# The second layer's feed-forward up projection by seven products instead of eight, with weight sums formed in DRAM

## The chip, the core and the metric

The kernel runs on one core of a Trainium2 chip. The metric is the device time of one execution in microseconds, lower is better; the kernel before has a median of 3490.95 us over three runs (3489.8 to 3501.07).

## What is computed

One inference step of a two-layer decoder trunk, for 1024 prompt tokens and 8 x 8 sample tokens (1088 in all, `NT`). Each layer mixes tokens, adds an output projection, and adds a gated feed-forward part with a causal convolution over three tokens on the gate. All arrays are float32. The part that the change touches is this one, and the first layer's copy of it runs beside the new weight sums:

```python
D_MODEL = 1024; D_FF = 2816; CONV_W = 3

def conv_glu(xn, conv_prev, w_up, conv_w, conv_b, w_down):
    T = xn.shape[1]
    u = xn @ w_up                                   # w_up: 1024 x 5632
    gate, val = u[..., :D_FF], u[..., D_FF:]
    ext = jnp.concatenate([conv_prev.astype(gate.dtype), gate], axis=1)
    conv = conv_b
    for j in range(CONV_W):
        conv = conv + ext[:, j:j + T] * conv_w[j]
    h = jax.nn.silu(conv) * val
    return h @ w_down, ext[:, T:]

# in trunk, for each layer l
        x = x + jnp.concatenate([o_tok, o_mem], axis=-1) @ P['w_o'][l]
        f, c = conv_glu(rms_norm(x, P['norm_ffn'][l]), conv0[l], P['w_ffn_up'][l],
                        P['conv_w'][l], P['conv_b'][l], P['w_ffn_down'][l])
        x = x + f
    y = rms_norm(x, P['final_norm'])
```

## The kernel before

The activations stay in SBUF with channels on partitions: `s.x` is 8 blocks (`KC`) of 128 channels by 1088 tokens. Every float32 product is made of three TensorE (PE) products: both operands are split into a rounded high part (fp32r) and a remainder, and `gemm_y` (L468 to L476) issues, for each block k of 128 input channels, wh·xh (L474), wh·xl (L475) and wl·xh (L476), all into one PSUM tile. The tokens are walked in three groups `G3` of 364, 364 and 360 columns, one PSUM bank each.

Weights come by `load_w` (L195 to L209): one DMA of 128x512 (256 KB) on SyncE's queue (SP, L204) into a ring `wr` of three buffers, a rounding copy `wh` on ScalarE (ACT, L207), and the remainder `wl` on VectorE (DVE, L208) into rings of four. An SP row waits until its `wr` buffer is free, and all weight loads stand in one line on SP.

`trunk_tail(l)` (from L1405) is the same code for both layers: output projection with w_o (loads of `od`, the attention's output in DRAM, through GpSimd's queue at L1427, split at L1433 and L1434), norm, `ffn` (from L1247), and for layer 1 `final`, the last norm with transposes and stores. The layers are numbered 0 and 1 in the code; the words "first" and "second" layer are used here. In `ffn` the 2816 hidden channels are 22 chunks c of 128. `up(c)` makes gate and value of a chunk (8 blocks x 3 groups x 3 products each), copies the gate from PSUM into `ext` (L1278), applies the convolution (L1300 to L1302), SiLU (L1303), the product with the value (L1317) and the split of the hidden tile into `hh` and `hl` (L1130, L1131). `down(i)` multiplies a group of three or four chunks by the down weights and adds to `s.x` (L1159); it is interleaved with the `up` of the following chunks (a merge by numbers of steps: 24 of `down` against 110 of `up`), and the last group runs alone in token pieces of 416, 416 and 256 in the second layer, beside `final`. Outside the few stretches marked for manual order, a scheduler sets each engine's order from the order of the code and an estimate of its own. Layers are run one after the other, with the second layer's attention between them: `trunk_tail(0)`, `attention`, `trunk_tail(1)`.

## Time and profile before

| | |
|---|---|
| median of three runs | 3490.95 us |
| the profiled execution | 3513.38 us |
| its span | 3511.6 us |
| PE busy | 3368.6 us (96%) |
| DVE, ACT, POOL busy | 1790.5, 1298.7, 457.7 us |
| first layer's feed-forward part | from about 1100 to 1840 us |
| second layer's last part (output projection to the end) | 2594.2 to 3511.6 us |

The profile is of one execution that took 3513.38 us, 0.6% above the median; shares and durations are read from it. It is read by stages: windows give the busy time of every engine in a stretch, and the waits of PE say what it lacked. Starts of successive matmuls are more exact than their durations, since ends of pipelined matmuls are modelled.

### The profile page before, as it was taken

Reading aid. Unit: us, or ns where it says so; the run is one execution under the profiler, and the core shown is the slowest. Engines: PE = TensorE matmul, PEld = TensorE weight load, DVE = VectorE, ACT = ScalarE, POOL = GpSimd, SP = SyncE. Lnnn points to the kernel's source line nnn. Section 1 sums busy time; section 2 is a strip of 40 time slices with the busy share of each in tenths; the row PEclk is TensorE's granted clock in tenths of the full one; section 3 lists DMA queues with packets and bytes.
Section 4 is the critical chain, followed back from the end, with each engine's and each line's share of the span. In section 5 each row is a group of like instructions: output and inputs, shape, how many; then the busy total and the mean of one; then the engine's idle time right before and its main releaser. Section 6 shows DMA issues by size and latency. Waiting matters only on the chain. (4 is left out here: it accounts for less than half of the span.)

```text
span 3511.6 us, 58202 instructions
## 1 busy us (share of the span) xinstructions
PE 3368.6 (96%) x23112; PEld 2899.4 (83%) x23112; DVE 1790.5 (51%) x4242; ACT 1298.7 (37%) x2971; POOL 457.7 (13%) x767
## 2 busy tenths in 40 slices
PE   6999999999889999999999999899999999999998
PEld 5555677775579999999999888655579999999998
DVE  5776676775535343333345477434445433343344
ACT  5555445543544222212225455333334312222222
POOL 4323133331011000000003001011111000000000
PEclk9998699998889999999999999899999999999999
DMA  4212011113141111111113102345321111111112
GB/s 119 56 39 76 22 39 41 38 47 95 51 153 48 43 49 43 43 46 46 44 46 111 53 28 70 123 163 179 121 75 42 49 49 40 46 46 43 47 44 78
DMA packets 299284, 227.13 MB, mean 65 GB/s; under 512 B 40890, under 2 KB 278222, under 8 KB 294916
## 3 DMA queue, kind: packets, MB, share of 16 engines
q1 hardware_dynamic: 285220, 166.82, 16.3%
q0 software_dynamic: 9888, 51.93, 4.2%
q10 hardware_dynamic: 3904, 4.65, 0.4%
q8 instruction: 182, 2.98, 0.3%
q14 instruction: 90, 0.74, 0.1%
HBM read 197.59 MB, written 25.76 MB: 64 GB/s over the span
## 5 line engine op out<-in xcount | busy, mean ns | idle before, releaser
L474 PE MATMUL pmm<-xh,wh 128*128 128x364 f32 (+2 forms) x2664 | 882.3, 331 | 7.5 <-ACT wh L207 4.8
L476 PE MATMUL pmm<-xh,wl 128*128 128x364 f32 (+2 forms) x2664 | 875.1, 328 | 0.0
L475 PE MATMUL pmm<-xl,wh 128*128 128x364 f32 (+2 forms) x2664 | 872.9, 328 | 0.3
L474 PEld LDWEIGHTS pmm<-xh,wh 128*128 128x128 f32 (+1 forms) x2664 | 500.1, 188 | 12.4 <-ACT wh L207 5.1
L475 PEld LDWEIGHTS pmm<-xl,wh 128*128 128x128 f32 (+1 forms) x2664 | 500.6, 188 | 3.0 <-DVE xl L1434 0.8
L476 PEld LDWEIGHTS pmm<-xh,wl 128*128 128x128 f32 (+1 forms) x2664 | 500.8, 188 | 1.4 <-DVE wl L208 0.2
L207 ACT CAST wh<-wr 128x512 fp32r<-128x512 f32 (+3 forms) x399 | 238.5, 603 | 561.1 <-PE pmm L475 333.4
L208 DVE TENSOR_TENSOR wl<-wr,wh 128x512 fp32r<-128x512 f32 (+2 forms) x307 | 205.0, 670 | 369.9 <-ACT wh L207 369.3
L1159 DVE TENSOR_TENSOR x<-x,pdn 128x364 f32<-128x364 f32 (+1 forms) x240 | 127.4, 531 | 419.2 <-PE pdn L476 419.2
L476 PE MATMUL pdn<-hh,wl 128*128 128x364 f32 (+1 forms) x912 | 300.2, 329 | 0.0
L475 PE MATMUL pdn<-hl,wh 128*128 128x364 f32 (+1 forms) x912 | 298.7, 328 | 0.0
L474 PE MATMUL pdn<-hh,wh 128*128 128x364 f32 (+1 forms) x912 | 298.3, 327 | 0.0
L474 PE MATMUL pmm<-xn,wh 128*128 128x292 f32 (+2 forms) x552 | 207.0, 375 | 3.7 <-DVE e L504 3.7
L475 PE MATMUL pmm<-xn,wh 128*128 128x292 f32 (+2 forms) x552 | 196.9, 357 | 0.0
L476 PE MATMUL pmm<-xn,wl 128*128 128x292 f32 (+2 forms) x552 | 195.5, 355 | 0.6 <-POOL wl L208 0.6
L1278 ACT COPY ext<-pmm 128x364 f32<-128x364 f32 x132 | 58.7, 444 | 364.0 <-PE pmm L476 364.0
L1304 POOL COPY cout<-ext 128x2 f32<-128x2 f32 x44 | 16.9, 385 | 1261.2 <-ACT ext L1278 1261.2
L476 PEld LDWEIGHTS pdn<-hh,wl 128*128 128x128 f32 x912 | 171.3, 188 | 1.1
L475 PEld LDWEIGHTS pdn<-hl,wh 128*128 128x128 f32 x912 | 171.3, 188 | 0.0
L474 PEld LDWEIGHTS pdn<-hh,wh 128*128 128x128 f32 x912 | 171.2, 188 | 0.0
L208 POOL TENSOR_TENSOR wl<-wr,wh 128x512 fp32r<-128x512 f32 (+1 forms) x92 | 121.7, 1325 | 195.9 <-ACT wh L207 163.8
L474 PEld LDWEIGHTS pmm<-xn,wh 128*128 128x128 f32 (+1 forms) x552 | 106.5, 193 | 27.9 <-issue 11.0
(720 smaller groups left out, 5984.1 us busy)
## 6 DMA issues: line engine op xcount, KB each, us to landing
wr<-in_w_ffn_up SPq DMA_DIRECT2D x176, 256.0 KB
wr<-in_w_in_a SPq DMA_DIRECT2D x84, 256.0 KB
wr<-in_w_ffn_down SPq DMA_DIRECT2D x64, 256.0 KB
wr<-in_w_o SPq DMA_DIRECT2D x32, 256.0 KB
wr<-in_w_ffn_down SPq DMA_DIRECT2D x32, 192.0 KB
xl<-odp POOLq DMA_DIRECT2D x4, 1456.0 KB
e<-in_x_prompt SPq DMA_DIRECT2D x16, 256.0 KB
out_y_p<-xl SPq DMA_DIRECT2D x8, 512.0 KB
```

The lines of the kernel that those rows point to most:

```text
L207: nc.scalar.copy(wh[:, :n, :m], wr[:, :n, :m])
L208: s.wl_eng.tensor_tensor(wl[:, :n, :m], wr[:, :n, :m], wh[:, :n, :m].bitcast(F32), ALU.subtract)
L474: nc.tensor.matmul(ps[:m, :n], wh[:, :m], xh[:, c0:c0 + n], start=(k == 0), stop=False)
L475: nc.tensor.matmul(ps[:m, :n], wh[:, :m], xl[:, c0:c0 + n], start=False, stop=False)
L476: nc.tensor.matmul(ps[:m, :n], wl[:, :m], xh[:, c0:c0 + n], start=False, stop=(k == last))
L1159: nc.vector.tensor_tensor(xv, xv, p[:, :n], ALU.add)
L1278: nc.scalar.copy(ext[:, 2 + c0:2 + c0 + m], p[:, :m])
L1304: nc.gpsimd.tensor_copy(cout[:, c, 0:2], ext[:, 1024:1026])
```

## The change

Write the up weights of the second layer as four quarters: the upper and the lower 512 input channels of gate and value, g1, g2, v1, v2 (each 512 x 2816), and cut the normed activations x in the same way into an upper part of four blocks (k = 0 to 3) and a lower one (k = 4 to 7), and the tokens of a half (`HT` = 544) into two quarters (`QT` = 272). The product of such a two-by-two arrangement takes eight quarter products. The change makes it from seven, with sums and differences of quarters as operands, and sums of the seven results (Winograd's form of Strassen's method).

- **Weight sums** (`sum_weights`, after L1247). Four arrays of 512 x 2816 in DRAM: vg = v1 + g1, gg = g1 + g2, vgg = vg + g2, all = vgg + v2. Each is made by four plain DMAs (rows in 128s, 1.44 MB each) on SP's queue that copy the first term, and four accumulating DMAs on GpSimd's queue that add the second. The 32 DMAs are stepped along the chunks of the first layer's `ffn`, one after an even chunk and two after an odd one.
- **Operands** (`combine_x`). For each half and each j of 0 to 3 the two normed blocks j and j + 4 (two DVE instructions of 544 columns), four differences on GpSimd (POOL, 272 columns), and the split of seven operands (seven ACT copies and seven DVE differences of 272). The first half's run beside the output projection, the second half's beside `down(0, 4)`.
- **Up** (`up` in `Seven`). 22 chunks x 2 halves, each seven products of 4 blocks x 3 matmuls of 272 columns. Seven weight tiles of 128x512 per chunk and half (`load_up`: three plain quarters, four sums from DRAM) through a ring `wa` of seven, with rings of five for the split parts. The results are put together from PSUM by two ACT copies, five DVE and two POOL instructions of 272. Convolution, SiLU, value product and split then run on 544 columns, with the first of the three convolution steps on ACT.
- **Output projection and down** run over quarters of 272 columns instead of three groups, down in groups of 4, 4, 4, 5 and 5 chunks per half, so the down weights are loaded once per half. The last `down` and `final` are walked by quarters of the second half.
- The first layer's own arithmetic is not changed. The new DMAs stand in its queues.

```diff
--- before.py
+++ after.py
+HT = NT // 2
+QT = NT // 4
+G4 = [(QT * i, QT) for i in range(4)]
...
+    def sum_weights(s, l):
+        nc, W = s.nc, s.I["w_ffn_up"][l]
+        S = s.wsum[l] = {z: s.t(s.dp, [512, DFF], f"ws{l}{z}", 1) for z in ("vg", "gg", "vgg", "all")}
+        def move(z, src, **kw):
+            eng = nc.gpsimd if kw else nc.sync
+            for r in range(0, 512, 128):
+                s.tc.keep_in_program_order(eng.dma_start(out=S[z][r:r + 128], in_=src[r:r + 128], **kw))
+                yield
+        def add(z, src):
+            return move(z, src, accum_op=ALU.add, max_dma_last_dim=5632)
+        g1, g2, v1, v2 = (W[r:r + 512, f:f + DFF] for f in (0, DFF) for r in (0, 512))
+        yield from s.seq(move("vg", v1), move("gg", g1), add("vg", g1), add("gg", g2), move("vgg", S["vg"]),
+                         add("vgg", g2), move("all", S["vgg"]), add("all", v2))
...
         groups = [(0, 4), (4, 4), (8, 4), (12, 4), (16, 3), (19, 3)]
+        sums = s.sum_weights(1)
...
                 yield from up(c, hs[i])
+                if l == 0:
+                    for _ in range(1 + c % 2):
+                        next(sums, None)
...
-        s.trunk_tail(1, od, xd, None, xst)
+        Seven(s).trunk_tail(1, od, xd, None, xst)
+
+
+class Seven(Step):
...
+    def residual(s, d, g, p, acc):
+        nc = s.nc
+        c0, n = g
+        xv = s.x[:, d, c0:c0 + n]
+        nc.vector.tensor_tensor(xv, xv, p[:, :n], ALU.add)
+        if acc is None:
+            return
+        a = acc[c0]
+        if d == 0:
+            nc.scalar.activation(a, xv, AF.Square)
+        else:
+            sq = s.st([128, QT], "nt", s.ntb)
+            nc.scalar.activation(sq[:, :n], xv, AF.Square)
+            nc.gpsimd.tensor_tensor(a, a, sq[:, :n], ALU.add)
...
+    def combine_x(s, h, gain, xs):
+        nc = s.nc
+        xs += [s.new_xq() for _ in range(7)]
+        lo, hi = slice(0, QT), slice(QT, HT)
+        for j in range(4):
+            a = []
+            for k in (j, j + 4):
+                a.append(s.st([128, HT], "tw", 2))
+                nc.vector.scalar_tensor_tensor(a[-1], s.x[:, k, HT * h:HT * h + HT], s.pv(gain[0], gain[1] + k), s.rstd[h], ALU.mult, ALU.mult)
+            yield
+            t = [s.st([128, QT], "nt", s.ntb) for _ in range(4)]
+            nc.gpsimd.tensor_tensor(t[0], a[0][:, hi], a[0][:, lo], ALU.subtract)
+            nc.gpsimd.tensor_tensor(t[1], a[1][:, hi], t[0], ALU.subtract)
+            nc.gpsimd.tensor_tensor(t[2], a[0][:, hi], a[1][:, hi], ALU.subtract)
+            nc.gpsimd.tensor_tensor(t[3], a[1][:, lo], t[1], ALU.subtract)
+            src = (a[0][:, lo], t[1], t[0], t[2], t[3], a[1][:, hi], a[1][:, lo])
+            for (xh, xl), z in zip(xs, src):
+                s.split(xh[:, j], xl[:, j], z)
+                yield
...
+    def gemm_x(s, wf, xs, h, acc=None, tag="dn"):
+        for d in range(KC):
+            w = wf(d)
+            for i in range(2):
+                p = s.pst(tag)
+                s.drain(s.gemm_y(p, w, xs[i], 0, QT))
+                s.residual(d, G4[2 * h + i], p, acc)
...
+    def load_up(s, l, c, first=False):
+        nc, W = s.nc, s.I["w_ffn_up"][l]
+        fv, fg = DFF + 128 * c, 128 * c
+        S = s.wsum[l]
+        for i, (src, r, f) in enumerate(((W, 0, fv), (S["vgg"], 0, fg), (S["gg"], 0, fg), (S["vg"], 0, fg), (W, 512, fg), (S["all"], 0, fg), (W, 512, fv))):
+            w = s.t(s.wp, [128, 4, 128], "wr", 3) if first and i < 3 else s.st([128, 4, 128], "wa", s.WA)
+            nc.sync.dma_start(out=w, in_=src[r:r + 512, f:f + 128].rearrange("(k p) f -> p k f", p=128))
+            wh, wl = (s.t(s.up, [128, 4, 128], z, 5, F32R) for z in ("uh", "ul"))
+            nc.scalar.copy(wh, w)
+            nc.vector.tensor_tensor(wl, w, wh.bitcast(F32), ALU.subtract)
+            yield [(wh[:, k], wl[:, k]) for k in range(4)]
...
+        def up(h, c, xs, out):
+            ws = s.load_up(l, c, h == c == 0)
+            ext = s.st([128, EW], "ext", 1)
+            es = ext[:, EW - 80:].rearrange("p (b t) -> p b t", t=10)
+            if h:
+                nc.gpsimd.tensor_copy(ext[:, 0:2], cout[:, c, 0:2])
+                nc.gpsimd.tensor_copy(es[:, :, 0:2], cprev[:, c].rearrange("p (b j) -> p b j", j=2))
+            else:
+                nc.gpsimd.memset(ext[:, 0:2], 0.0)
+            def product(i):
+                p = s.pst("mm")[:, :QT]
+                w, (xh, xl) = next(ws), xs[i]
+                for k in range(4):
+                    wh, wl = w[k]
+                    nc.tensor.matmul(p, wh, xh[:, k], start=k == 0, stop=False)
+                    nc.tensor.matmul(p, wh, xl[:, k], start=False, stop=False)
+                    nc.tensor.matmul(p, wl, xh[:, k], start=False, stop=k == 3)
+                    yield
+                return p
+            nt = lambda: s.st([128, QT], "nt", s.ntb)
+            add = lambda eng, o, a, b, op=ALU.add: eng.tensor_tensor(o, a, b, op)
+            V, P = nc.vector, nc.gpsimd
+            p = yield from product(0)
+            t1 = nt()
+            nc.scalar.copy(t1, p)
+            p = yield from product(1)
+            u2 = nt()
+            add(V, u2, p, t1, ALU.subtract)
+            p = yield from product(2)
+            t5 = nt()
+            nc.scalar.copy(t5, p)
+            p = yield from product(3)
+            u3 = nt()
+            add(V, u3, p, u2)
+            if h:
+                m = NP_ - 3 * QT
+                add(P, ext[:, 2 + QT:2 + QT + m], u3[:, :m], t5[:, :m])
+                b8 = lambda z: z[:, m:].rearrange("p (b t) -> p b t", t=8)
+                add(P, es[:, :, 2:10], b8(u3), b8(t5))
+            else:
+                add(P, ext[:, 2 + QT:2 + HT], u3, t5)
+            p = yield from product(4)
+            add(V, ext[:, 2:2 + QT], p, u3)
+            add(P, t5, t5, u2)
+            L = EW - 2 if h else HT
+            cv = s.st([128, EW], "cv", 1)[:, :L]
+            w = [s.pv(f"conv_w{l}{j}", c) for j in range(3)]
+            nc.scalar.activation(cv, ext[:, 0:L], AF.Identity, scale=w[0], bias=s.pv(f"conv_b{l}", c))
+            nc.vector.scalar_tensor_tensor(cv, ext[:, 1:1 + L], w[1], cv, ALU.mult, ALU.add)
+            nc.vector.scalar_tensor_tensor(cv, ext[:, 2:2 + L], w[2], cv, ALU.mult, ALU.add)
+            nc.scalar.activation(cv, cv, AF.Silu)
+            if h:
+                nc.gpsimd.tensor_copy(cout[:, c, 0:2], ext[:, EW - 82:EW - 80])
+                nc.gpsimd.tensor_copy(cout[:, c, 2:18].rearrange("p (b j) -> p b j", j=2), es[:, :, 8:10])
+            else:
+                nc.gpsimd.tensor_copy(cout[:, c, 0:2], ext[:, HT:HT + 2])
+            t = s.st([128, HT], "tw", 2)
+            p = yield from product(5)
+            add(V, t[:, QT:], p, t5, ALU.subtract)
+            p = yield from product(6)
+            add(V, t[:, :QT], p, t1)
+            hh, hl = s.st([128, HT], "hh", 7, F32R), s.st([128, HT], "hl", 7, F32R)
+            out.append((hh, hl))
+            if h:
+                V.tensor_tensor(t[:, :QT + m], cv[:, :QT + m], t[:, :QT + m], ALU.mult)
+                sv = s.bc(cv[:, EW - 80:EW - 79], [10, 8], [1, 8])
+                V.tensor_tensor(b8(t[:, QT:]), sv, b8(t[:, QT:]), ALU.mult)
+            else:
+                V.tensor_tensor(t, cv, t, ALU.mult)
+            s.split(hh, hl, t)
+            yield
...
+        groups = [(0, 4), (4, 4), (8, 4), (12, 5), (17, 5)]
+        hs, acc0, squares = {}, {}, []
...
+        def ups(h, i):
+            c0, n = groups[i]
+            hs[h, i] = []
+            if h and i == 0:
+                yield from s.combine_x(1, ("norm_ffn", 8 * l), operands[1])
+            for c in range(c0, c0 + n):
+                if h == 0 and c == 1:
+                    normed()
+                if h == 0 and c == 4:
+                    earlier()
...
+                yield from up(h, c, operands[h], hs[h, i])
...
+        def down(h, i):
+            yield from s.gemm_x(lambda d: wd(i, d), quarters(hs.pop((h, i))), h)
...
+        order = [(h, i) for h in range(2) for i in range(len(groups))]
+        for n, z in enumerate(order):
+            u = ups(*z)
+            if n:
+                s.merge([(down(*order[n - 1]), 16), (s.take(u, 64), 64)])
+            s.drain(u)
...
+                def first_x():
+                    for _ in range(4):
+                        yield
+                    normed(0)
+                    yield from s.combine_x(0, ("norm_ffn", 8 * l), xs)
+                with s.tc.manual_schedule(engines={mybir.EngineType.Activation, mybir.EngineType.DVE}):
+                    ws[0] = w(0)
+                    s.drain(parts(os_[0]))
+                    ws[1] = w(1)
+                if l == 0:
+                    s.drain(s.load_x(first))
+                s.merge([(s.gemm_x(w, os_[0], 0, accs[0], "mm"), 16), (parts(os_[1]), 16)])
+                s.merge([(s.gemm_x(w, os_[1], 1, accs[1], "mm"), 16), (first_x(), 36)])
...
```

Three places show what the scheduler makes of this. The first is the SP queue in the first layer's feed-forward part (`wr` is a weight load, `ws1gg` one of the four sums). Before:

```order
L204 DMA wr_12930<-in_w_ffn_up 128x4x128
L204 DMA wr_13025<-in_w_ffn_up 128x4x128
L204 DMA wr_13031<-in_w_ffn_up 128x4x128
L204 DMA wr_13127<-in_w_ffn_down 128x4x128
L204 DMA wr_13147<-in_w_ffn_up 128x4x128
L204 DMA wr_13153<-in_w_ffn_up 128x4x128
L204 DMA wr_13232<-in_w_ffn_down 128x4x128
L204 DMA wr_13324<-in_w_ffn_up 128x4x128
L204 DMA wr_13330<-in_w_ffn_up 128x4x128
```

and after, at the same chunks:

```order
L207 DMA wr_12932<-in_w_ffn_up 128x4x128
L207 DMA wr_12938<-in_w_ffn_up 128x4x128
L207 DMA wr_13033<-in_w_ffn_up 128x4x128
L207 DMA wr_13039<-in_w_ffn_up 128x4x128
L1255 DMA ws1gg_12519<-in_w_ffn_up 128x2816 x2
L207 DMA wr_13137<-in_w_ffn_down 128x4x128
L207 DMA wr_13157<-in_w_ffn_up 128x4x128
L207 DMA wr_13163<-in_w_ffn_up 128x4x128
L207 DMA wr_13242<-in_w_ffn_down 128x4x128
L207 DMA wr_13334<-in_w_ffn_up 128x4x128
L207 DMA wr_13340<-in_w_ffn_up 128x4x128
```

Two copies of 1.44 MB stand ahead of the following weight loads, which were in an unbroken row before. The second place is DVE inside the second layer, where `up` runs without `down`: about one chunk of 1088 tokens before (`wl` is a weight remainder, `cv` the convolution, `nt` and `hl` the hidden tile),

```order
L208 TENSOR_TENSOR wl_28888<-wr_28885,wh_28887 128x512
L1300 TENSOR_SCALAR cv_28770<-ext_28688,ptile_198_728 128x1104
L1301 SCALAR_TENSOR_TENSOR cv_28770<-ext_28688,ptile_198_728,cv_28770 128x1104
L1302 SCALAR_TENSOR_TENSOR cv_28770<-ext_28688,ptile_198_728,cv_28770 128x1104
L1317 TENSOR_TENSOR nt_28816<-cv_28770,pmm_28791 128x364
L1131 TENSOR_TENSOR hl_28790<-nt_28816,hh_28789 128x364
L1317 TENSOR_TENSOR nt_28845<-cv_28770,pmm_28820 128x364
L1131 TENSOR_TENSOR hl_28790<-nt_28845,hh_28789 128x364
L208 TENSOR_TENSOR wl_28983<-wr_28980,wh_28982 128x512
L1317 TENSOR_TENSOR nt_28874<-cv_28770,pmm_28849 128x296
L1320 TENSOR_TENSOR nt_28874<-cv_28770,pmm_28849 128x64
L208 TENSOR_TENSOR wl_28989<-wr_28986,wh_28988 128x512
```

and part of one chunk of 544 tokens after (`ul` is a weight remainder, `nt`, `ext` and `tw` take results from PSUM, `pmm`):

```order
L2435 TENSOR_TENSOR ul_27918<-wa_27915,uh_27917 128x512
L2435 TENSOR_TENSOR ul_27945<-wa_27942,uh_27944 128x512
L2485 TENSOR_TENSOR nt_27863<-pmm_27844,nt_27821 128x272
L2435 TENSOR_TENSOR ul_27966<-wa_27963,uh_27965 128x512
L2485 TENSOR_TENSOR ext_27779<-pmm_27866,nt_27863 128x272
L2435 TENSOR_TENSOR ul_27987<-wa_27984,uh_27986 128x512
L2514 SCALAR_TENSOR_TENSOR cv_27887<-ext_27779,ptile_198_728,cv_27887 128x544
L2485 TENSOR_TENSOR tw_27893<-pmm_27894,nt_27842 128x272
L2515 SCALAR_TENSOR_TENSOR cv_27887<-ext_27779,ptile_198_728,cv_27887 128x544
L2485 TENSOR_TENSOR tw_27893<-pmm_27914,nt_27800 128x272
L2435 TENSOR_TENSOR ul_28008<-wa_28005,uh_28007 128x512
L2534 TENSOR_TENSOR tw_27893<-cv_27887,tw_27893 128x544
```

DVE now has a PSUM row or a weight remainder for nearly every product, in half the tokens. The third place is DVE where the second half begins, which has no counterpart before, since the kernel had no halves (`xl` are the operands' remainders of `combine_x` for j = 2, `x` with `pdn` the additions of `down`, `wl` a weight of the same `down`):

```order
L2381 SCALAR_TENSOR_TENSOR tw_32386<-x_22950,ptile_195_718,rstd_26140 128x544
L2324 TENSOR_TENSOR x_22950<-x_22950,pdn_32369 128x272
L2381 SCALAR_TENSOR_TENSOR tw_32388<-x_22950,ptile_195_718,rstd_26140 128x544
L1134 TENSOR_TENSOR xl_32229<-tw_32386,xh_32228 128x272
L1134 TENSOR_TENSOR xl_32233<-nt_32390,xh_32232 128x272
L2324 TENSOR_TENSOR x_22950<-x_22950,pdn_32404 128x272
L1134 TENSOR_TENSOR xl_32239<-tw_32388,xh_32238 128x272
L1134 TENSOR_TENSOR xl_32231<-nt_32391,xh_32230 128x272
L1134 TENSOR_TENSOR xl_32235<-nt_32392,xh_32234 128x272
L1134 TENSOR_TENSOR xl_32237<-nt_32393,xh_32236 128x272
L1134 TENSOR_TENSOR xl_32241<-tw_32388,xh_32240 128x272
L211 TENSOR_TENSOR wl_32432<-wr_32429,wh_32431 128x512
```

The last row, a weight that `down`'s fourth block of output channels waits for, comes to stand behind the operands of j = 2.

## Rows read from the trace of the kernel before

**Rows 1.** The page's first part: engine, busy us (share), instructions.

```profile
PE 3368.6 (96%) x23112; PEld 2899.4 (83%) x23112; DVE 1790.5 (51%) x4242; ACT 1298.7 (37%) x2971; POOL 457.7 (13%) x767
```

**Rows 2.** Windows by stretch: engines' busy us, granted clock, DMA share, GB/s.

```profile
core 0: us, PE busy (x) PEld busy (x) DVE busy (x) ACT busy (x) POOL busy (x), PEclk, DMA share, GB/s
1250.00:1300.00 50.00, 50.00 (x304) 49.89 (x303) 19.59 (x34) 9.72 (x18) 1.08 (x4) 1.00 0.17 48
2750.00:2800.00 50.00, 50.00 (x303) 50.00 (x302) 20.61 (x33) 13.92 (x26) 1.55 (x8) 1.00 0.17 49
2850.00:2900.00 50.00, 50.00 (x304) 50.00 (x303) 17.72 (x29) 9.41 (x17) 1.08 (x4) 1.00 0.15 44
```

**Rows 3.** Waits of PE from 2590 us to the end: us, times, longest.

```profile
PE pmm L474 <- ACT wh L207: 4.8, 1, 4.8
PE pmm L474 <- ACT xh L1433: 1.6, 1, 1.6
PE pmm L1488 <- DVE x L1159: 0.5, 1, 0.5
```

**Rows 4.** Chain of waits around 2600 us: start, us, what.

```profile
2598.46 10.50 DMA wr<-in_w_o
2608.99 0.63 ACT wh L207
2609.66 0.67 PE pmm L474
```

**Rows 5.** PE's timeline: start, us, instruction; half clock, then 416 and 256 columns.

```profile
2611.76 0.51 PE L474 MATMUL pmm<-xh,wh 128*128 128x364 f32 x1
2613.58 0.39 PE L474 MATMUL pmm<-xh,wh 128*128 128x364 f32 x1
...
3466.95 0.35 PE L474 MATMUL pmm<-hh,hh 128*128 128x416 f32 x1
3469.75 0.35 PE L474 MATMUL pmm<-hh,wh 128*128 128x416 f32 x1
...
3492.08 0.28 PE L475 MATMUL pmm<-hl,hh 128*128 128x256 f32 x1
3493.88 0.28 PE L475 MATMUL pmm<-hl,hh 128*128 128x256 f32 x1
```

**Rows 6.** Groups by shape, 2750 to 3400 us (POOL 2640 to 2720): busy, mean ns, idle.

```profile
L208 DVE TENSOR_TENSOR wl<-wr,wh 128x512 fp32r<-128x512 f32 x104 | 71.9, 691 | 126.9 <-ACT wh L207 126.8
L1159 DVE TENSOR_TENSOR x<-x,pdn 128x364 f32<-128x364 f32 x74 | 39.4, 532 | 125.8 <-PE pdn L476 125.8
L1301 DVE SCALAR_TENSOR_TENSOR cv<-ext,ptile,cv 128x1104 f32<-128x1104 f32 x18 | 24.6, 1369 | 0.6
L1131 DVE TENSOR_TENSOR hl<-nt,hh 128x364 fp32r<-128x364 f32 x36 | 19.4, 538 | 20.3 <-ACT hh L1130 20.3
L207 ACT CAST wh<-wr 128x512 fp32r<-128x512 f32 x104 | 64.1, 620 | 191.8 <-PE pmm L475 114.3 <-PE pdn L475 72.0 <-ACT ext L1280 3.9
L1303 ACT ACTIVATE cv<-cv 128x1104 f32<-128x1104 f32 x18 | 20.3, 1128 | 67.1 <-DVE cv L1302 67.1
L1278 ACT COPY ext<-pmm 128x364 f32<-128x364 f32 x37 | 17.3, 466 | 168.7 <-PE pmm L476 168.7
L1168 POOL TENSOR_TENSOR acc<-acc,nt 128x364 f32<-128x364 f32 x8 | 8.2, 1024 | 25.9 <-ACT nt L1167 25.9
```

**Rows 7.** DVE's and POOL's timeline around 1870 us: start, us, instruction.

```profile
1867.77 0.52 DVE L1159 TENSOR_TENSOR x<-x,pmm 128x364 f32<-128x364 f32 x1
1868.21 0.68 DVE L1131 TENSOR_TENSOR wl<-wr,wh 128x512 fp32r<-128x512 f32 x1
1868.81 0.53 DVE L1131 TENSOR_TENSOR xl<-x,xh 128x364 fp32r<-128x364 f32 x1
...
1878.58 1.09 DVE L1131 TENSOR_TENSOR xl<-x,xh 128x364 fp32r<-128x364 f32 x1 [0.58 <-ACT xh L1130]
...
1878.31 2.21 POOL L1168 TENSOR_TENSOR cv<-cv,nt 128x364 f32<-128x364 f32 x2 [1.58 <-ACT nt L1167]
```

**Rows 8.** SP's and ACT's timeline in the first layer's feed-forward part.

```profile
1324.27 2.32 SPq L204 DMA_DIRECT2D wr<-in_w_ffn_up  x2
...
1336.77 0.62 ACT L207 CAST wh<-wr 128x512 fp32r<-128x512 f32 x1 [1.33 <-PE pmm L475]
```

**Rows 9.** DMA view of 2590 to 2660 us: GB/s in 40 slices; queue, packets, MB, share.

```profile
GB/s 0 75 112 0 125 342 376 360 360 288 263 41 0 179 121 0 0 0 0 0 0 0 0 9 0 0 0 0 0 150 36 159 105 150 150 97 133 80 144 156
...
q1 hardware_dynamic: 7664, 3.80, 19.8%
```

## The prediction on record

> **What bounds the kernel now.** I read the shares first, then the stages by windows, then PE's waits and the chain at the one place where PE stops, and last single starts. PE is busy 96% of the span, DVE 51% [rows 1]. In the feed-forward windows PE is busy all of 50 us, at granted clock 1.00 (the 2.4 GHz level), with 303 or 304 matmuls, in the first layer as in the second [rows 2]. So both are bound by PE, and one matmul costs 50 / 303.5 = 0.1647 us at a mean width of 1088 / 3 = 362.7 columns. DVE is busy some 35 to 41% there, ACT 19 to 28%, and the DMA engines 15 to 17%. From 2590 us to the end PE waits for others 6.9 us in all, 4.8 of it once [rows 3]: a w_o load issued at 2598.46 lands 10.5 us later [rows 4], in the slices in which the DMA view shows 342 to 376 GB/s [rows 9], which are the loads of `od`. After that wait PE ran at the 1.2 GHz level from 2609.66 to 2613.58: two starts there, with five matmuls between them, are 1.82 us apart, 0.303 each [rows 5]. So nothing but PE's own work sets the end of this stage, and what the change takes from PE counts in full until another engine or a queue is late.
>
> **PE's work.** A matmul costs its columns and something fixed: fifteen spacings of 416 columns take 2.80 us, 0.187 each, and fifteen of 256 take 1.80, 0.120 each [rows 5]. At 2.4 columns per ns that leaves 13.3 to 13.6 ns per matmul beside the columns, and 13.6 at 362.7 columns too. For 272 columns the line between them gives 0.1267 us. Each of these matmuls has a weight load of its own, before and after.
>
> Before: output projection 8 x 8 x 3 x 3 = 576, up 44 x 8 x 3 x 3 = 3168, down of 19 chunks 19 x 8 x 9 = 1368, so 5112 x 0.1647 = 841.9 us; last down 72 x (0.187 + 0.187 + 0.120) = 35.6. Sum 877.5. After: output projection 8 x 8 x 4 x 3 = 768, up 22 x 2 x 7 x 12 = 3696, down 22 x 8 x 4 x 3 = 2112, so 6576 x 0.1267 = 833.2. **Difference -44.3 us.** Up alone goes from 521.8 to 468.3 (-53.5), where seven of eight would be -65: the narrower matmuls give back 12 us, and the other two parts lose 9.
>
> The rows show 13.3 to 13.6 ns per matmul beside the columns [rows 5]. The Trainium skill's page "TensorE: Matmul & The Clock Gate", section "Wait — 56ns, not 53.3ns?", has start to start as N / 2.4 GHz plus about 2.5 ns. By it the stage would go from 818 to 762 us, -57; the trace disagrees for these fp32r matmuls, and the rows decide.
>
> **VectorE in up.** A chunk and half is 84 matmuls, 10.64 us of PE. DVE has in it seven weight remainders of 128x512 at 0.691; five PSUM rows of 272 at about 0.44 (0.532 for 364, less 92 columns at the 1.12 ns per column between the 364 and the 1104 rows); two convolution steps, one product and one remainder of 544 columns at about 0.74 (0.538 for 364 plus 180 columns) [rows 6]: 4.84 + 2.2 + 2.96 = 10.0 us. Starts in an unbroken row are nearer than durations: 0.60 for 0.68, 0.44 for 0.52 [rows 7], 0.085 less for each of 16, so 8.6. POOL adds two instructions of about 1.024 x 272 / 364 = 0.77 us [rows 6], and a DVE instruction with two SBUF operands took 1.09 beside a POOL addition where its like took 0.53 [rows 7]; two of them held by 0.3 to 0.55 add 0.6 to 1.1. So 9.2 to 9.7 by pitches, up to 11.1 by durations, against 10.64. I take the pitches, since in such a row DVE is never idle between instructions. Beside `down` there is room: 4 chunks' down work is 24 us of PE with 12.6 of DVE. About 25 of the 44 chunk halves run without it (a merge takes 64 of the steps of `up`, a little over two chunks). **Taken +2 us, bounds 0 to 12** (25 x 0.46 at 11.1). What is dearer than that is a rival.
>
> ACT has seven casts at 0.62, two copies near 0.4, two passes of 544 near 0.6 and a cast near 0.6, about 7 us [rows 6]. Weights are 7 x 256 KB = 1.84 MB per 10.64 us, 172 GB/s; the `od` loads were moved at 342 to 376 [rows 9]. Both are hidden as long as the loads keep ahead: the ring of seven raw tiles and five split ones is some 12 products deep, 18 us.
>
> **Start of the stage.** The operands of the second half get buffers of their own, and the first half's loads are 272 columns wide, so the w_o load has less ahead of it. The 4.8 us and the slower 3.92 us (13 matmuls at 0.303 for 0.165, 1.8 us) can both go, or a wait of the same size can stay: **-5, bounds -6.6 to 0.** Next late is the split of the first tiles, 1.6 us before [rows 3]; it stays.
>
> **Start of up.** The first `wa` loads can only be issued when the output projection's buffers at that place are free, and stand behind `down`-type rows on SP; three first tiles use `wr`. No row shows this. Nearest is a w_o load's 10.5 us [rows 4] against a lead of three products, 4.6 us, so up to 8: **+3, bounds 0 to 8;** no gain, since PE waited for nothing there [rows 3].
>
> **Half switch.** `combine_x(1)` is 8 DVE instructions of 544, 28 remainders of 272 and 16 POOL differences: 8 x 0.74 + 28 x 0.44 + 16 x 0.77 = 5.9 + 12.3 on DVE and 12.3 on POOL, in four rounds of about 4.7 us each, beside `down(0, 4)`, which has 5 x 8 x 4 / 2 x 3 = 240 matmuls, 30.4 us. DVE work in that stretch is 18 + 16 additions + 16 weight remainders, 36 us with the held ones, so DVE is just too long, and a `down` weight remainder is queued behind the round j = 2 (the third place of the order); PE's in-order row waits for it. **+5, bounds 1 (a single wait) to 12** (36 less 30, doubled by rows in bad order and a stretch at half clock).
>
> **End.** Quarters of 272 make the last stretch after the last matmul a little shorter or longer than the 14 us now: **+2, bounds -2 to 4.** `normed(1)` changes ACT's function once or twice in c = 1, beside matmuls with operands ready: **+1, 0 to 2.**
>
> **First layer.** Its arithmetic is the same. Added are 16 plain moves of 1.44 MB on SP's queue ahead of weight loads, and 16 accumulating ones on POOL, which has 1 us of work in 50 there [rows 2]. Each moved pair stands between two weight loads (first place of the order). A load issued at 1324.27 is cast at 1336.77, 12.5 us later [rows 8], and `wh` has three more tiles in hand, 10 us: some 20 us of slack by this estimate. A move reads and writes 1.44 MB; at the 342 GB/s of the `od` loads [rows 9] that is 4.2 us one way, a pair 8.4, within the slack; at half of it a pair takes 17, still within. The DMA engines are busy 15 to 17% there [rows 2]; 32 x 1.44 MB over 500 us is 92 GB/s more. No row shows a move from DRAM to DRAM or an accumulating DMA. **+1, bounds 0 to 12** (one stall of a pair at half the rate); no gain, since PE is busy 50 of 50 us there.
>
> The Trainium skill's "SBUF — State Buffer", section "🔬 SBUF: two separate sides", says that the port pair shared by DVE and GpSimd is an exclusive lock: a DVE instruction with two SBUF inputs and a POOL one that reads SBUF hold each other for the whole instruction. The trace agrees: 1.09 us beside a POOL addition, 0.53 without. The PSUM rows are not held, 0.52 both times.
>
> **Sum.** -44.3 + 2 - 5 + 3 + 5 + 2 + 1 + 1 = -35 us. The profiled execution took 3513.4, 0.6% above the median; the same microseconds come off either, the cause of the 0.6% being unknown. 3490.95 - 35 = **3456 us**; 3478 for an execution like the profiled one. With all terms at their good bounds it is 3439, at their bad ones 3490.95 - 44 + 50 = 3497, which no one mishap gives.
>
> **Rivals.**
> *A, as forecast.* For it: PE full for 50 of 50 us [rows 2], which leaves the arithmetic.
> *B, DVE becomes the bound* in the 25 chunk halves without `down`. For: 10.0 us by durations before any hold [rows 6], and rows held by POOL [rows 7]. Against: pitches. It decides from 10.64 us per chunk half. If every POOL instruction holds two DVE rows in full (4 x 0.56) over the durations, 12.3: 25 x 1.7 = 42 us, so 3456 + 42 = 3498, no change. By the lock rule of that page a POOL instruction can also be kept out by DVE's row and its chain come late; the time would be the same 3498.
> *C, slower: moves stop the first layer's weights.* SP's queue is in order and a move of the third and fourth sum waits on SP for POOL's additions; `wr` loads behind them then come late. For: SP is in front of all weight loads [rows 8]. Against: 20 us of slack. It decides from about 20 us for a pair. At 70 GB/s a pair takes 41, and the four pairs that the order shows cost 20 us each beyond the slack: +80, so 3535.
> *D, dearer seams.* The starts and the switch at their upper bounds (8, 12), and each stop followed by a stretch at 0.303 for 0.165 as in [rows 5]: +22, 3478.
>
> **How the numbers follow.** A 0.60, D 0.13, B 0.14, C 0.13. A and D leave out 0.27, so the range takes in B and ends at 3498; below, at 3439, with the good bounds. What measurement can tell from no change is 0.3%, 10.5 us: faster is below 3480.5 (A and D, 0.73), the same is B (0.14), slower is C (0.13).
>
> **What would show it.** Right: 272-column spacings near 0.127 at granted clock 1.00, some 395 matmuls in a 50 us window of the second layer, DVE at 75 to 90% there, no 4.8 us wait at the first w_o matmuls, one group of waits of PE for DVE at the half switch, and 303 or 304 matmuls per 50 us still in the first layer. Wrong: PE waits for `ul` in the chunks between the merges (B), PE waits for `wh` in the first layer while SP waits for a DMA (C), or a spacing of 272 columns above 0.135, which alone would take back 55 us and with it the gain.

## The result, and the profile after

The changed kernel takes 3460.98 us (median of five, 3457.89 to 3468.17) against 3490.95: a ratio of 0.9908, interval 0.9884 to 0.9932, so 30 us faster by the medians and some 32 by the ratio, near the 3456 of the forecast. The profiled execution took 3465.75 us, its span is 3464.0, 47.6 below that of before. Of this, 12.4 lie ahead of the second layer's output projection (first w_o matmul at 2594.18 before, 2581.73 after), though PE, DVE and ACT have the same instructions in the same order up to there; another execution of the changed kernel has its first w_o matmul at 2592.71, and over the traces of all kernels with the new second layer, which run the same code up to there, it lies between 2571.1 and 2600.2. That part is not the change's. From the first w_o matmul to the end it is 917.4 us before and **882.3 after: -35.1**, which is what the forecast was made for; this "last part" is used below, since it does not carry what happens earlier.

The page's first part and the windows of after (columns as in [rows 1] and [rows 2]):

```profile
PE 3314.6 (96%) x24362; PEld 2844.6 (82%) x24362; DVE 2060.9 (59%) x4790; ACT 1502.6 (43%) x3355; POOL 633.3 (18%) x982
```

```profile
1250.00:1300.00 50.00, 50.00 (x304) 49.89 (x303) 21.02 (x36) 10.57 (x19) 2.33 (x5) 1.00 0.41 108
2750.00:2800.00 50.00, 50.00 (x400) 50.00 (x399) 36.91 (x65) 23.50 (x41) 7.54 (x12) 1.00 0.52 153
2850.00:2900.00 50.00, 49.77 (x396) 49.55 (x395) 39.90 (x70) 25.52 (x45) 7.86 (x12) 1.00 0.49 144
```

The first layer (1250 to 1300 us) has its 304 matmuls still, with the DMA engines at 41% for 17. The second layer is full of PE again, with some 398 narrow matmuls for 304, and DVE has gone from about 40% to 74 and 80% of these windows, which hold stretches with and without `down`. Where PE is not full, the windows of 10 us show it (a full one has 82 matmuls):

```profile
2650.00:2660.00 10.00, 7.33 (x59) 7.11 (x58) 8.88 (x15) 5.98 (x15) 5.11 (x7) 1.00 0.08 25
2690.00:2700.00 10.00, 4.75 (x29) 3.68 (x27) 4.59 (x10) 3.96 (x10) 2.55 (x4) 0.90 0.66 196
2700.00:2710.00 10.00, 10.00 (x63) 9.78 (x63) 6.96 (x14) 9.86 (x15) 2.09 (x4) 0.75 0.86 252
...
3030.00:3040.00 10.00, 9.81 (x76) 9.37 (x75) 9.01 (x15) 6.34 (x11) 4.17 (x6) 1.00 0.50 144
3040.00:3050.00 10.00, 7.93 (x57) 7.26 (x57) 8.87 (x17) 4.15 (x13) 4.91 (x5) 1.00 0.21 61
3050.00:3060.00 10.00, 7.68 (x50) 6.59 (x51) 10.00 (x19) 5.12 (x13) 5.65 (x7) 1.00 0.09 26
3060.00:3070.00 10.00, 8.23 (x61) 7.54 (x60) 9.32 (x19) 6.16 (x16) 4.16 (x4) 1.00 0.14 41
```

The first three are the start of up, the others the half switch. PE's longest waits from 2580 us to the end, where before had those of [rows 3]:

```profile
PE pmm L477 <- ACT xh L2662: 3.3, 2, 2.5
PE pmm L2478 <- ACT uh L2434: 3.2, 1, 3.2
PE pmm L479 <- DVE wl L211: 2.7, 1, 2.7
PE pdn L477 <- DVE x L2324: 1.9, 3, 1.3
PE pdn L477 <- ACT hh L1133: 1.7, 8, 0.2
```

**The sum with measured terms.** The matmuls missing from 82 in each short window, times their spacing, give PE's loss in a place: 12.6 us at the start of up (2640 to 2720), 10.6 at the half switch, 5.7 in the first 24 us of the stage, and about 2 in the rest. In the trace of the second execution of the changed kernel the start of the stage takes 3.4, the start of up some 1 us more and the half switch some 1.5 more; so a place's loss is known from one trace to about 2 us, and smaller differences between runs say little. A spacing of 272 columns is 0.1258 us (548.5 us of busy PE in 2740 to 3000 and 3110 to 3400 us, 4358 matmuls), and one of 362.7 columns before was 0.1657, taken over 650 us instead of 50.

| term of the sum | forecast | measured |
|---|---|---|
| PE's matmuls, 6576 x 0.1258 for 5112 x 0.1657 + 35.6 | -44.3 | -55 |
| start of the stage (5.7 for 7.5) | -5 | -1.8 |
| start of up | +3 (0 to 8) | +12.6 |
| half switch | +5 (1 to 12) | +10.6 |
| VectorE in up, the stretches without down | +2 | 0 |
| PE's waits for ACT's `hh` as each `down` starts (1.7 in 8 waits) | 0 | +2 |
| end, after the last feed-forward matmul (13.7 for 14.6) | +2 | -0.9 |
| the second half's norm | +1 | in the start of up |
| not placed, transposes among it | 0 | -2.6 |
| last part | -36 | -35.1 |
| first layer | +1 | +2.5 |

### The profile page after: what moved, and what is told of

Its sections match the earlier page's. It is cut to its first block, busy times and chain, and to the rows that moved or that the text cites. A ratio compares the mean times of both kernels' runs of the same rounds, so it can differ in the third digit from the quotient of the medians.

```text
span 3464.0 us, 63205 instructions
## 1 busy us (share of the span) xinstructions
PE 3314.6 (96%) x24362; PEld 2844.6 (82%) x24362; DVE 2060.9 (59%) x4790; ACT 1502.6 (43%) x3355; POOL 633.3 (18%) x982
## 5 line engine op out<-in xcount | busy, mean ns | idle before, releaser
L477 PE MATMUL pmm<-xh,wh 128*128 128x364 f32 (+3 forms) x1544 | 509.0, 330 | 4.4 <-ACT xh L2662 3.3
L479 PE MATMUL pmm<-xh,wl 128*128 128x364 f32 (+3 forms) x1544 | 503.6, 326 | 0.0
L478 PE MATMUL pmm<-xl,wh 128*128 128x364 f32 (+3 forms) x1544 | 503.3, 326 | 0.2
L2478 PE MATMUL pmm<-xh,uh 128*128 128x272 f32 x1232 | 357.1, 290 | 4.7 <-ACT uh L2434 3.2
L2479 PE MATMUL pmm<-xl,uh 128*128 128x272 f32 x1232 | 355.9, 289 | 1.6 <-DVE xl L1134 1.6
L2480 PE MATMUL pmm<-xh,ul 128*128 128x272 f32 x1232 | 356.8, 290 | 0.0
L477 PE MATMUL pdn<-hh,wh 128*128 128x272 f32 (+2 forms) x1080 | 329.4, 305 | 3.6 <-DVE x L2324 1.9
L479 PE MATMUL pdn<-hh,wl 128*128 128x272 f32 (+2 forms) x1080 | 328.5, 305 | 0.8 <-DVE wl L211 0.8
L478 PE MATMUL pdn<-hl,wh 128*128 128x272 f32 (+2 forms) x1080 | 328.3, 305 | 0.3 <-DVE hl L1134 0.3
L2479 PEld LDWEIGHTS pmm<-xl,uh 128*128 128x128 f32 x1232 | 232.9, 189 | 2.2 <-DVE xl L1134 2.2
```

Source lines behind the costliest of these rows:

```text
L477: nc.tensor.matmul(ps[:m, :n], wh[:, :m], xh[:, c0:c0 + n], start=(k == 0), stop=False)
L478: nc.tensor.matmul(ps[:m, :n], wh[:, :m], xl[:, c0:c0 + n], start=False, stop=False)
L479: nc.tensor.matmul(ps[:m, :n], wl[:, :m], xh[:, c0:c0 + n], start=False, stop=(k == last))
L2478: nc.tensor.matmul(p, wh, xh[:, k], start=k == 0, stop=False)
L2479: nc.tensor.matmul(p, wh, xl[:, k], start=False, stop=False)
L2480: nc.tensor.matmul(p, wl, xh[:, k], start=False, stop=k == 3)
```

## The experiments

Each run is a kernel of its own; spans of the last part are from one trace of each, ratios against the kernel before on the same chip. The intervals of the ratios of all changed kernels overlap that of the first, so what single edits do is read from the last part and its places alone.

| run | last part, us | ratio and interval |
|---|---|---|
| kernel before | 917.4 | |
| changed kernel, and again | 882.3, 883.1 | 0.9908; 0.9892 (0.9858 to 0.9927) |
| sums_only | 918.3 | 1.0026 (1.0004 to 1.0047) |
| no_second_operands | 872.1 | 0.9883 (0.9859 to 0.9907) |
| wa_own_place | 880.3 | 0.9927 (0.9902 to 0.9951) |
| up_loads_first | 886.1 | 0.9933 (0.9911 to 0.9955) |
| norm_later | 879.5 | 0.9866 (0.9838 to 0.9894) |
| norm_later_only | 882.1 | 0.9899 (0.9859 to 0.9939) |
| diffs_on_dve | 879.1 | 0.9876 (0.9848 to 0.9903) |
| up_adds_on_dve | 879.4 | 0.9868 (0.9841 to 0.9896) |
| combined | 870.6 | 0.9875 (0.9848 to 0.9901) |
| comb_slow | **866.2** | 0.9860 (0.9828 to 0.9892) |
| comb_both | 871.3 | 0.9880 (0.9845 to 0.9915) |

**Are the weight sums free?** The new first layer with the old second one:

```diff
-        Seven(s).trunk_tail(1, od, xd, None, xst)
+        s.trunk_tail(1, od, xd, None, xst)
```

> The kernel before with the 32 DMAs of the weight sums along its first feed-forward part, and the second layer as before (the sums are made and not read). Theory (the sums are free, since the first layer's weight loads have some 20 us in hand): within 4 us of the kernel before, 303 or 304 matmuls in each 50 us window from 1250 to 1800 us, and a second layer's last part of 917 us from its first w_o matmul to the end, as before. Rival (the DMAs hold up weight loads, or what follows them): 5 to 12 us slower than before, with windows under 300 matmuls.

Windows of 303 and 304 matmuls throughout (1250 to 1850 us), also where the DMA engines are at 65%. SyncE did wait for transfers in the changed kernel, 13.7 us in three waits where before had 0.9, and PE did not once before the layer's end, so the slack of [rows 8] was enough. One wait is new, as the layer ends, and both kernels with the sums have it (PE's waits in 1840 to 1900 us: before, changed, sums_only):

```profile
PE pdn L1393 <- ACT cvst L1395: 0.4, 2, 0.2
```

```profile
PE pdn L1418 <- ACT cvst L1420: 2.9, 2, 2.7
```

```profile
PE pdn L1418 <- ACT cvst L1420: 3.0, 2, 2.8
```

That is 2.5 us. It is rival C on a small scale: the last accumulating DMA is issued at 1849.05, the DMA engines' share is 0.93 and 1.04 in the two windows from 1850 to 1860 us (0.27 and 0.15 before), and ACT, whose later copies PE waits for, sits idle for a down weight for 4.2 us, where before its waits of this kind were 2.0 us in all:

```profile
1861.18 1.59 ACT L1133 CAST hh<-wr 128x384 fp32r<-128x384 f32 x3 [4.16 <-DMA wr<-in_w_ffn_down]
```

No run moved this DMA, so the chain is read from the trace and not tested. The ratio, 1.0026, is some 9 us with an interval from 1 to 16. What is beyond 2.5 does not lie beside the DMAs before that: from PE's 9000th to its 13000th matmul (1155 to 1818 us in before), both kernels take 662.8 us. Stretches that no edit touches scatter by more (the 15000th to the 16000th matmul, in the second layer's attention, takes 168 to 182 us over all traces). So the rest stays open. Rival C's price of 80 us did not come.

**The half switch.** First its price, with the second half's products fed by the first half's operands:

```diff
-                yield from s.combine_x(1, ("norm_ffn", 8 * l), operands[1])
+                operands[1] = operands[0]
```

> The second half's products take the first half's operands, so combine_x(1) is left out with its 8 normed blocks, 16 differences and 28 splits; the second half of the output is therefore not the layer's. Theory (what PE loses at the half switch, 73 matmuls of 317 in 3030 to 3070 us, 9 us, is VectorE's time for these operands): those four 10 us windows are full again at about 80 matmuls each, and the last part goes from 882.3 to about 873 us. Rival (it is lost by the switch itself, by weight loads or the order on PE's queue): more than 4 of the 9 us stay.

The last part is 10.2 us shorter, and the windows from 3040 us are full: these operands are the whole loss. Next the GpSimd differences in them, moved to VectorE (`nc.gpsimd` to `nc.vector` in four lines):

> The sixteen differences of combine_x per half go from GpSimd to VectorE, which has 7 us more of its own work at the half switch (16 x 0.44). Theory (VectorE's rows with two SBUF operands were held by GpSimd's differences there: 28 remainders of 272 took 673 and 563 ns against some 430 unheld, about 5 us, and some 2 us on other rows): the remainders fall to about 440 ns, VectorE's total stays, and the last part is 878 to 883 us. Rival (the two engines worked side by side): VectorE's 7 us come on top, remainders keep their time, 887 to 890 us.

Groups by shape on VectorE at the half switch (3030 to 3072 us), changed kernel and this one:

```profile
L1134 DVE TENSOR_TENSOR xl<-nt,xh 128x272 fp32r<-128x272 f32 x16 | 10.2, 673 | 1.8 <-ACT xh L1133 1.8
L1134 DVE TENSOR_TENSOR xl<-tw,xh 128x272 fp32r<-128x272 f32 x12 | 6.7, 563 | 0.0
```

```profile
L1134 DVE TENSOR_TENSOR xl<-nt,xh 128x272 fp32r<-128x272 f32 x16 | 6.2, 435 | 0.0
L1134 DVE TENSOR_TENSOR xl<-tw,xh 128x272 fp32r<-128x272 f32 x12 | 4.9, 434 | 0.0
```

The remainders fall from 673 and 563 to 435 ns, 5.8 us in all, and the loss from 10.6 to 7.4. So VectorE was held by GpSimd, as in [rows 7]. By the sum of its operand rows VectorE gained nothing (24.2 us in 36 rows, then 25.3 in 52, with 7.0 for the differences); yet from the first of these rows to the last it takes 27.7 us for 31.0, since its idle time there (1.8 us, for ACT's `xh` of GpSimd's differences) is gone and the rows of others between them are fewer. Whether the hold or the shorter chain through GpSimd counts for more was not tested. VectorE was busy 10 of 10 us there, which spoke for too much work; the last runs tested that.

**Is VectorE nearly the bound in up?** GpSimd's additions there on VectorE as well (`V = P = nc.vector`):

> GpSimd's additions of 272 columns per chunk and half in up go to VectorE (two or three instructions, some 0.9 to 1.1 us per 10.6 us). VectorE is busy 37 to 39 of 50 us in the stretches without down, so it has room for this by the theory: 882 within 2 us, its busy share up by 3 us in 50 or less. Rival (rival B of the prediction: VectorE is nearly the bound there): 20 us or more are added over the 25 chunk halves without down, 900 us or more.

Windows of 3110 to 3400 us, changed kernel and this one:

```profile
3110.00:3400.00 290.00, 289.16 (x2294) 288.28 (x2294) 215.46 (x399) 139.60 (x247) 65.35 (x123) 1.00 0.48 140
```

```profile
3110.00:3400.00 290.00, 289.82 (x2300) 288.94 (x2299) 224.43 (x453) 138.69 (x247) 19.97 (x70) 1.00 0.48 139
```

VectorE takes 9 us more in 290 and PE stops less than before. But the 77% is a mean over stretches with and without `down`, and so are the 37 to 39 of 50 us that the expectation gives to the stretches without. Where PE runs no `down` matmul for 20 us or more, VectorE is busy 84 to 88%, and 87 to 90% with the additions; one such stretch, changed kernel and this one:

```profile
3300.00:3327.00 27.00, 27.00 (x216) 27.00 (x215) 22.77 (x42) 16.87 (x30) 10.38 (x18) 1.00 0.61 175
```

```profile
3298.00:3325.00 27.00, 27.00 (x216) 27.00 (x215) 24.04 (x51) 16.64 (x30) 2.67 (x10) 1.00 0.61 175
```

PE has the same 216 matmuls and no stop in either: rival B did not come, but there is a tenth of VectorE left and not a quarter. The last part, 879.4, is below the 882 within 2 of the expectation; 1.3 us of that lie at the start of the stage, which the edit does not touch.

**The start of up.** Three theories, three edits: a place of their own for the raw up weights (an unused tile under them), their first loads kept ahead of seven down weights on SyncE's queue, and the second half's norm held behind the third chunk.

```diff
+                s.lay(([128, 512 * s.WA], "pad", 1), ([128, QT], "nt", s.ntb), ...)
...
+            if first:
+                s.tc.keep_in_program_order(q)      # q: the load in load_up
...
-                if h == 0 and c == 1:
+                if h == 0 and c == 3:               # normed(), its instructions kept in order
```

> Only the place in memory of the raw up weights changes: an unused tile of the same size is laid under them in the output projection's pool, so that no buffer of that stage has to be free before the first of these loads. Two theories for the stop of PE before the fourth product (2693 to 2699.5 us; with the slower clock after it some 8 us): by the first, the loads wait for the buffers of the output projection, and the stop shrinks from 3.2 us at that product to under 1 us, the last part from 882.3 to about 877. By the second, they wait behind seven down weights in SyncE's queue, the last of them issued at 2694.7, and nothing changes: 882 within 1.5 us.

The fourth product still waits 3.0 us for 3.2, since its load is issued at 2695.69 for 2695.27: not the buffers. Of the 2 us that the last part is shorter, 1.5 lie at the start of the stage (4.2 for 5.7), where the second execution of the changed kernel also lost less. SyncE's queue in the changed kernel shows what stands ahead of that load:

```profile
2683.11 11.98 SPq L207 DMA_DIRECT2D wr<-in_w_ffn_down  x7
2695.27 0.37 SPq L2432 DMA_DIRECT2D wa<-ws1vg  x1
```

> As the run with the raw up weights in a place of their own, and the first chunk's seven weight loads kept in the order of the code on SyncE's queue, so that they stand ahead of the seven down weights. By the second theory (queue order) the fourth product starts without a stop, PE keeps the 2.4 GHz level there, and the last part is 875 to 878 us; what is left of the loss is VectorE's share in 2650 to 2660 us, about 2.7 us. If neither buffers nor queue order are the cause (then VectorE is, which forms the operands until 2690), the last part stays above 880.

A miss: the loads go out at 2682.7, 13 us earlier, and the last part is 4 us longer. ACT's timeline shows what came in their way (`rstd` from `pdn` is the norm, `uh<-wr` the first casts of up weights):

```profile
2691.33 0.49 ACT L2366 ACTIVATE rstd<-pdn,eps 128x272 f32<-128x272 f32 x1 [0.72 <-PE pdn L2365]
2691.72 0.42 ACT L2332 ACTIVATE nt<-x 128x272 f32<-128x272 f32 x1
2694.40 0.49 ACT L2366 ACTIVATE rstd<-pdn,eps 128x272 f32<-128x272 f32 x1 [2.26 <-PE pdn L2365]
2694.91 1.28 ACT L2369 ACT_TABLE_LOAD   x1
2696.20 0.66 ACT L2369 ACTIVATE rstd<-rstd 128x544 f32<-128x544 f32 x1
2696.76 1.64 ACT L2436 CAST uh<-wr 128x512 fp32r<-128x512 f32 x3
```

The norm of the second half, which nobody needs for 300 us, was put ahead of the first casts of up weights; it waits for PE, PE for the last squares, and the casts stand behind it. So:

> As up_loads_first, and the second half's norm (mean matmuls, Ln and Exp) is held in the order of the code and moved behind the third chunk. Theory: what stopped PE in up_loads_first was this norm, which the scheduler had put ahead of the first casts of up weights on ACT and ahead of the first products on PE, where it waited for the last squares. Without it PE runs through the start of up: no stop longer than 1 us between 2680 and 2700 us, and the last part takes 874 to 877 us (up_loads_first 886.1, the changed kernel 882.3). Rival (VectorE, busy with the first operands until 2690, is the cause): 880 or more.

> Only the second half's norm is moved behind the third chunk; up weights and down weights stay in the changed kernel's order. If norm and queue order each stop PE there, the stops of 0.5 and 1.6 us at the mean matmuls go and the fourth product still waits for its weight, issued near 2695 us: 879 to 881 us. If the norm alone is the cause, 874 to 877.

With both edits the wait for `uh` is 1.6 us and the loss at this place 9.0 for 12.6; the norm alone gives nothing (882.1, over its 879 to 881), since then the queue order stops the fourth product for 5.1 us (PE's waits in norm_later_only and in norm_later):

```profile
PE pmm L2478 <- ACT uh L2434: 5.1, 1, 5.1
```

```profile
PE pmm L2480 <- ACT uh L2436: 1.6, 1, 1.6
```

PE's stops at the mean matmuls and at `uh` add up to 5.3 us in the changed kernel, 6.3 with the up weights first, 5.1 with the norm later, and 1.6 with both: each of the two hid the other. With 879.5 norm_later met neither its forecast, 874 to 877, nor its rival, 880 or more. It is 3 us over the forecast: the stop at `uh` stayed at 1.6 us where under 1 was expected, VectorE's 2.7 us wait for `wl` near 2650 stayed, and here PE went to the 1.2 GHz level after it (46 matmuls at granted clock 0.83, for 59 at 1.00 in the changed kernel), which is nearly 2 us that comes and goes between executions.

**Together, and the order at the half switch.**

> The changed kernel once more, for a time on the same chip as the runs below: 0.988 to 0.993 of the kernel before, last part 882 us within 2.

> Norm later, up weights first, differences and additions on VectorE together. The single steps gave a last part of 879.5 (norm later with up weights first), 879.1 (differences) and 879.4 us (additions) against 882.3. If they act in different places they add up: 873 to 875 us, and the whole is 7 to 9 us below the changed kernel. If VectorE, which takes all of it, now becomes the bound in the stretches without down (37 to 39 of 50 us busy before), or at the half switch, less than half of this comes: 878 or more.

870.6, 2.4 below the forecast's range: start of up 6.9 us, half switch 7.1. VectorE bears it, and the single steps add up. PE's waits at the half switch (3010 to 3060 us):

```profile
PE pdn L479 <- DVE wl L211: 1.6, 2, 1.1
PE pmm L2481 <- DVE xl L1134: 0.8, 1, 0.8
PE pmm L2480 <- ACT xh L1133: 0.5, 1, 0.5
PE pdn L477 <- DVE x L2324: 0.3, 1, 0.3
```

The rest of the 7.1 us is stops too short for this list and the start again after each. Then the operands spread over all of `down`:

```diff
-                s.merge([(down(*order[n - 1]), 16), (s.take(u, 64), 64)])
+                k = 32 if z == (1, 0) else 64
+                s.merge([(down(*order[n - 1]), 16), (s.take(u, k), k)])
```

> As combined, and at the half switch 32 steps of the operands instead of 64 steps of operands and products are merged with the 16 of down, so that the operands are spread over all of it. Theory (VectorE has some 36 us of work in a stretch of 30 us of PE): the loss of 7 to 9 us there stays within 2 us. Rival (it is a matter of the order, additions of down behind rows of operands): the loss falls below 5 us.

Windows of the half switch, combined and comb_slow:

```profile
3020.00:3030.00 10.00, 9.60 (x73) 9.00 (x72) 10.00 (x23) 5.68 (x15) 0.00 (x0) 1.00 0.12 34
3030.00:3040.00 10.00, 7.99 (x50) 6.55 (x48) 10.00 (x28) 4.65 (x13) 0.00 (x0) 1.00 0.09 28
3040.00:3050.00 10.00, 9.05 (x67) 8.58 (x68) 9.96 (x26) 6.29 (x16) 0.00 (x0) 1.00 0.21 60
```

```profile
3030.00:3040.00 10.00, 9.61 (x73) 9.01 (x73) 9.95 (x21) 5.83 (x12) 0.32 (x2) 1.00 0.33 95
3040.00:3050.00 10.00, 10.00 (x82) 10.00 (x81) 9.82 (x26) 4.69 (x14) 0.00 (x0) 1.00 0.13 38
3050.00:3060.00 10.00, 10.00 (x82) 10.00 (x81) 9.96 (x26) 4.57 (x13) 0.00 (x0) 1.00 0.32 94
```

The theory falls. VectorE is just as full, but PE is too, and the loss is 1.1 us for 7.1. What stopped PE was the order: at 64 steps to 16 all operands fell into the first half of `down`, their rows stood ahead of the additions and weights that `down` needs, and PE, which is in order, waited. In the list of waits above, a weight of `down` is the largest and the additions the smallest, so the rival of this run is right in the order and not in what stood behind. Spread out, the excess of VectorE's work is carried into the chunks behind: VectorE stays 94 to 100% busy up to 3110 us, and PE has 81 or 82 matmuls in each window from 3040 to 3100 all the same. The edit also takes the products of up out of `down`'s second half; that was not tested apart.

> As comb_slow, and this one down takes PSUM tiles from the ring of six instead of that of two, so that PE need not wait for each of its additions on VectorE. Theory (VectorE's sum of work): PE's waits move from the additions to the weights and operands and the loss stays within 2 us of comb_slow. Rival (the two PSUM tiles stop PE): 3 us or more less.

7.7 us again, with waits for `wl` and `wh` of 1.7 and 1.5 us and a stretch at the 1.2 GHz level behind them (granted clock 0.66 in 3030 to 3040 us): more PSUM tiles let the scheduler order the rows otherwise, and worse. Both theories of this run fail by that; why the order turns, is open. comb_slow has the shortest last part, 866.2 for 882.3 and 883.1 in the two executions of the changed kernel; in whole time it has 3448.17 us against 3462.96 for the changed kernel on the same chip, with intervals that overlap, and combined has 3448.49, so the gain of comb_slow over combined stands in the traces alone.

## Why the forecast was right, and where it was not

- **What bounds the stage** was read rightly from [rows 2]: PE full, and the gain is PE's arithmetic. By the Trainium skill's page "TensorE: Matmul & The Clock Gate", section "Wait — 56ns, not 53.3ns?", an estimate gives -57, close to the measured -55; yet the trace disagrees with the rule itself, since 0.1258 us at 272 columns is 12.5 ns beside the columns and not 2.5. That it comes close is luck: it is too short by some 65 us for before and for after alike.
- **The term of the matmuls was mis-sized by 11 us.** Two steps: 50 us over 303.5 counts about two matmuls that straddle a window's ends, so before is 0.1657 and not 0.1647 (5 us), and the line between 256 and 416 columns [rows 5] gave 0.1267 for 0.1258 (6 us).
- **The start of the stage**: the w_o wait of [rows 4] did go, as argued. But PE came out of a 2.5 us wait for `xh` at the 1.2 GHz level (granted clock 0.60 in 2580 to 2590 us) and lost 5.7 where before lost 7.5, the 1.6 us for `xh` of [rows 3] counted in; the clause "can both go" held for the wait and not for the clock.
- **The start of up** was priced from one DMA's landing and came out beyond its bound of 8. It named the buffers, which wa_own_place excludes, and the rows ahead on SP, which is right. The step that failed is the norm of the other half: it was priced at +1 "beside matmuls with operands ready", and it stood ahead of the first casts on ACT and the first products on PE, in a row with the seven down weights on SyncE's queue (shown by the two runs together). VectorE's late `wl` and the slower clock behind the stops (0.90 and 0.75 in 2690 to 2710 us) were not in it.
- **The half switch** was within its bounds, at their upper end, with the wrong mechanism: not more VectorE work than PE time, but its order (comb_slow), and GpSimd's hold on it (diffs_on_dve). The `down` weight behind the operands, seen in the third place of the order, was the right row.
- **VectorE in up** was taken by pitches, rightly: 84 to 88% in the stretches without `down` is about 9.0 us for 84 matmuls, for the 9.2 to 9.7 of the forecast, and there was room for more (up_adds_on_dve). The +2 us taken for it did not come; the 2 us lost in those stretches are PE's waits for ACT's `hh`. Rival B is excluded by that run, rival C, but for 2.5 us, by sums_only; D is what in part happened: the two seams took 15 us more than taken, and the matmuls gave 11 back. That the total fits so closely is luck, the sum of these errors; that the kernel gains by PE's arithmetic is not.

## What to carry to other kernels

Fewer, narrower products paid here where PE was full for whole windows and the helpers stayed below full in the stretch that is tightest for them (VectorE 84 to 90%): count PE's pitch from long windows, and the helpers' share from that stretch alone and not from a mean over stretches of different kinds. The loss then sits at the seams, and there the order of work on in-order queues counts for more than its amount: look for what stands ahead of the first weights of a stage, and spread a burst of side work over everything that can hide it. Where a stop has several causes, mend them together as well as one by one, since one alone can show nothing.

## What was not expected of the hardware

- A GpSimd difference of 272 columns makes VectorE's remainders beside it half as long again (673 for 435 ns), and VectorE's stretch of operands became shorter when it took the differences over (27.7 for 31.0 us).
- Accumulating DMAs of 1.44 MB from DRAM to DRAM land in 11.2 to 14.4 us (medians of four) beside weight loads, with PE undisturbed but for 2.5 us at the layer's end.
- After the same wait of 2.7 us PE goes on at granted clock 1.00 (of a 10 us window) in one execution and at 0.83 to 0.88 in others, worth up to 2 us each time.
